# Gate and up projections of two SwiGLU feed-forwards as Strassen block products (seven multiplications for eight)

## The chip, the cores and the metric

One NeuronCore of a Trainium2 chip runs the whole program. The metric is device time in microseconds of one execution. The engines are TensorE (matmuls, "PE"; its weight loads are "PEld"), VectorE ("DVE"), ScalarE ("ACT"), GpSimd ("POOL") and SyncE ("SP", which here issues the DMAs).

## The reference

One layer on 512 prompt tokens and 8 x 8 sample tokens (576 in all), model width 1024, feed-forward width 2816, in float32:

```python
h = modulate(rms_norm(x, n1_g), sh1, sc1)
x = x + 0.5 * g1 * swiglu(h, w1_gate, w1_up, w1_down)
h = modulate(rms_norm(x, nm_g), sh2, sc2)
mix, S_new, v_rows = token_mix(h, pos0, S0, w_in, ..., w_a, w_b, w_o)
x = x + g2 * mix
h = modulate(rms_norm(x, n2_g), sh3, sc3)
x = x + 0.5 * g3 * swiglu(h, w2_gate, w2_up, w2_down)

def swiglu(h, w_gate, w_up, w_down):
    return (jax.nn.silu(h @ w_gate) * (h @ w_up)) @ w_down
```

The shifts, scales and gates (sh, sc, g) come from `silu(c) @ w_ada + b_ada`, nine vectors of 1024 per sequence. The token mix is a gated spatial MLP beside a retention, merged through w_a, w_b and w_o.

## The kernel before

Activations stand feature-major: 8 chunks k of 128 features by 576 tokens. The tokens are two halves h of H = 288. For float32 accuracy each operand is split into a high part (a cast to fp32r) and a low part (the rest): three matmuls, high-high, high-low, low-high. Weights come from HBM as raw blocks of 512 KB (`load_raw`, line 67, on SyncE's queue); `split_w` casts on ScalarE (all ScalarE work has line 96, a wrapper that can keep ScalarE in the order of the text) and subtracts on VectorE (line 77), for a few first weights on POOL. Raw, high and low tiles rotate through five buffers each.

`proj` (line 349) makes one product of 128 outputs by 288 tokens: 8 k x 3 matmuls of 128x128 by 128x288 into one PSUM bank. `ffn` runs over 22 chunks f of 128 columns in groups of 8, 6 and 8. For each chunk it makes gate and up for both halves (4 x 24 = 96 matmuls); `act` applies silu on ScalarE, multiplies on VectorE (line 412) and splits the result (line 85) into G. After a group, `w_down` is applied to its chunks (16 products) and `resid` (lines 335 to 341) adds to x. The norms of the next stage are accumulated as x becomes final, half 0 ahead of half 1 (`LAST`).

At the start, w_ada for the first shifts and scales is fetched in 32 blocks of 256 KB (`ada_first`, line 225); two features of h at a time are modulated, and the first three weights' projections take each feature as it is ready (`block`). The other 14 strips of w_ada (`ada_strip`; matmuls in line 180, transposes 191, loads 207) run as side work between FFN 1's products: `tick` lets a generator go on after so much main work.

Between the stages, x goes to HBM (x1d) and back, w_in's first weights are fetched ahead of the end of FFN 1 and spread among the x1d stores on SyncE, and w_o's follow w_a's. The scheduler orders each engine by the text and its priorities; a transfer starts when its buffer is free and those ahead of it on SyncE have been issued.

## Time and profile before

| | us |
|---|---|
| median of 3 runs | 1774.22 |
| runs | 1772.92, 1774.22, 1774.97 |
| span of the profiled execution (its total time was not taken) | 1771.8 |
| TensorE busy | 1743.8 |
| VectorE busy | 798.6 |
| ScalarE busy | 568.3 |
| GpSimd busy | 231.6 |

The profile is one execution, and its times count from the start of the span. A group's row has the line, engine, operation, output and inputs with their shapes and the count, then busy time, mean ns of one, and the idle time before it with what ended it. A row of the stretches has start:end and length, then busy time and count of PE, PEld, DVE, ACT and POOL (with a line chosen, PE and PEld alone), the granted TensorE clock, the DMA share and GB/s. In the chain and the timeline a row has start, length, engine and line.

### The profile page before, as it was taken

Reading aid. Unit: us, or ns where it says so; the run is one execution under the profiler, and the core shown is the slowest. Engines: PE = TensorE matmul, PEld = TensorE weight load, DVE = VectorE, ACT = ScalarE, POOL = GpSimd, SP = SyncE. Lnnn points to the kernel's source line nnn. Section 1 sums busy time; section 2 is a strip of 40 time slices with the busy share of each in tenths; the row PEclk is TensorE's granted clock in tenths of the full one; section 3 lists DMA queues with packets and bytes.
Section 4 is the critical chain, followed back from the end, with each engine's and each line's share of the span. In section 5 each row is a group of like instructions: output and inputs, shape, how many; then the busy total and the mean of one; then the engine's idle time right before and its main releaser. Section 6 shows DMA issues by size and latency. Waiting matters only on the chain.

```text
span 1771.8 us, 30817 instructions
## 1 busy us (share of the span) xinstructions
PE 1743.8 (98%) x13068; PEld 1675.5 (95%) x13068; DVE 798.6 (45%) x1409; ACT 568.3 (32%) x943; POOL 231.6 (13%) x282
## 2 busy tenths in 40 slices
PE   7999999999999999999999999999999999999997
PEld 4899998999999999999999889999999999999997
DVE  4532333333366557566655654412536333343332
ACT  4422122132243433333333333322334222222233
POOL 2000000000243123022112101420042000000011
PEclk9999999999999999999999999999999999999999
DMA  9555545562333334334323333332223322132211
GB/s 310 168 162 156 167 140 169 152 185 82 120 106 102 118 110 125 108 94 123 103 87 108 101 96 110 92 120 83 82 64 85 95 84 82 56 102 84 84 37 55
DMA packets 278109, 199.55 MB, mean 113 GB/s; under 512 B 8137, under 2 KB 252105, under 8 KB 277970
## 3 DMA queue, kind: packets, MB, share of 16 engines
q1 hardware_dynamic: 277970, 197.57, 37.3%
q8 instruction: 103, 1.69, 0.4%
q14 instruction: 36, 0.29, 0.1%
HBM read 183.12 MB, written 14.42 MB: 111 GB/s over the span
## 4 chain that ended last, share of the span: by engine, by line
PE 93%; DVE 2%; DMA 2%; ACT 1%; issue 1%; POOL 1%; SPq 0%; POOLq 0%; ACTq 0%; DVEq 0%
PE ps L349 75%; PE ps L609 5%; PE ps L825 3%; PE ps L180 2%; PE ps L739 1%; PE ps L617 1%; PE ps L701 1%; DMA wraw<-in_w_down_dram 1%; PE ps L745 1%; PE ps L717 0%; DVE h L304 0%; DVE XX L312 0%; PE ps L760 0%; PE ps L472 0%; PE ps L191 0%
## 5 line engine op out<-in xcount | busy, mean ns | idle before, releaser
L349 PE MATMUL ps<-XX,whi 128*128 128x288 f32 x4864 | 983.2, 297 | 8.3 <-ACT XX L96 5.8
L349 PEld LDWEIGHTS ps<-XX,whi 128*128 128x128 f32 x4864 | 781.0, 188 | 31.1 <-issue 13.4
L349 PE MATMUL ps<-XX,wlo 128*128 128x288 f32 x2432 | 718.7, 296 | 0.0
L77 DVE TENSOR_TENSOR wlo<-wraw,whi 128x1024 fp32r<-128x1024 f32 (+1 forms) x240 | 297.3, 1244 | 437.9 <-ACT whi L96 434.0
L349 PEld LDWEIGHTS ps<-XX,wlo 128*128 128x128 f32 x2432 | 456.9, 188 | 0.0
L349 PE MATMUL ps<-c,whi 128*128 128x288 f32 x2176 | 440.5, 297 | 0.0
L96 ACT CAST whi<-wraw 128x1024 fp32r<-128x1024 f32 (+1 forms) x248 | 255.3, 1035 | 544.7 <-PE ps L349 326.6
L349 PEld LDWEIGHTS ps<-c,whi 128*128 128x128 f32 x2176 | 348.0, 188 | 9.5 <-issue 6.7
L349 PE MATMUL ps<-c,wlo 128*128 128x288 f32 x1088 | 320.7, 295 | 0.0
L349 PEld LDWEIGHTS ps<-c,wlo 128*128 128x128 f32 x1088 | 204.2, 188 | 0.0
L341 POOL TENSOR_TENSOR x<-x,s 128x64 f32<-128x64 f32 x56 | 18.5, 331 | 929.2 <-DVE s L340 929.2
L412 DVE TENSOR_TENSOR h<-ps,h 128x288 f32<-128x288 f32 x88 | 40.2, 456 | 166.9 <-PE ps L349 165.6
L96 ACT CAST c<-h 128x288 fp32r<-128x288 f32 x120 | 51.5, 432 | 160.5 <-DVE h L412 139.9
L335 DVE SCALAR_TENSOR_TENSOR x<-ps,gate,x 128x288 f32<-128x288 f32 (+1 forms) x96 | 46.2, 482 | 120.6 <-PE ps L349 120.6
L609 PE MATMUL ps<-whi,XX 128*128 128x256 f32 x512 | 91.2, 281 | 0.0
L609 PEld LDWEIGHTS ps<-whi,XX 128*128 128x128 f32 x512 | 78.6, 188 | 0.0
L96 ACT COPY c<-ps 128x64 f32<-128x64 f32 (+3 forms) x86 | 37.0, 433 | 126.6 <-PE ps L609 72.1
L609 PE MATMUL ps<-wlo,XX 128*128 128x256 f32 x256 | 71.9, 281 | 0.0
L96 ACT ACTIVATE h<-ps 128x288 f32<-128x288 f32 x104 | 42.5, 409 | 79.2 <-PE ps L349 79.0
L85 DVE TENSOR_TENSOR c<-h,c 128x288 fp32r<-128x288 f32 x120 | 54.2, 454 | 25.0 <-ACT c L96 24.9
L794 DVE TENSOR_TENSOR c<-c,ps 128x288 f32<-128x288 f32 x112 | 46.4, 448 | 33.6 <-PE ps L349 33.2
L564 POOL TENSOR_TENSOR c<-h,h 128x288 f32<-128x288 f32 x32 | 33.3, 1042 | 191.2 <-DVE h L563 191.2
(176 smaller groups left out, 1279.8 us busy)
## 6 DMA issues: line engine op xcount, KB each, us to landing
wraw<-in_w_in_dram SPq DMA_DIRECT2D x80, 512.0 KB
wraw<-in_w_ada_dram SPq DMA_DIRECT2D x56, 512.0 KB
wraw<-in_w_gate_dram SPq DMA_DIRECT2D x44, 512.0 KB
wraw<-in_w_up_dram SPq DMA_DIRECT2D x44, 512.0 KB
wraw<-in_w_down_dram SPq DMA_DIRECT2D x32, 512.0 KB
c<-in_w_ada_dram SPq DMA_DIRECT2D x32, 256.0 KB
S<-in_state_ret_dram SPq DMA_DIRECT2D x32, 256.0 KB
wraw<-in_w_b_dram SPq DMA_DIRECT2D x16, 512.0 KB
```

What stands on the lines that cost most here:

```text
L77: (eng or DVE).tensor_tensor(out=lo, in0=raw, in1=hi.bitcast(F32), op=ALU.subtract)
L85: DVE.tensor_tensor(out=lo, in0=src, in1=hi.bitcast(F32), op=ALU.subtract)
L96: inst = f(*args, **kw)
L180: PE.matmul(ps[32 * g:32 * g + 32], lhsT=cs[:, k, :], rhs=w, start=k < 4, stop=k >= 4, tile_position=(0, 32 * g))
L335: DVE.scalar_tensor_tensor(out=x[:, o:o + w], in0=ps[:, :w], scalar=g[:, c, 0:1], in1=x[:, o:o + w], op0=ALU.mult, op1=ALU.add)
L341: POOL.tensor_tensor(out=x[:, NP:T], in0=x[:, NP:T], in1=u, op=ALU.add)
L349: PE.matmul(ps[:, :H], lhsT=s[:, k, c0:c0 + P], rhs=m[:, HALF[h]], start=k == 0 and z == 0, stop=k == kc - 1 and z == 2,)
L412: DVE.tensor_tensor(out=g, in0=pu[:, :H], in1=s, op=ALU.mult)
L564: POOL.tensor_tensor(out=dst[:, HALF[h]], in0=t1, in1=t2, op=ALU.add)
L609: PE.matmul(ps[:, :DV], lhsT=s, rhs=m, start=i == 0, stop=i == 23)
L794: DVE.tensor_tensor(out=dst, in0=dst, in1=ps[:, :H], op=ALU.add)
L825: PE.matmul(ps, lhsT=s, rhs=m[:, kx % 2, :], start=kx == 0 and z == 0, stop=kx == KC - 1 and z == len(terms) - 1,)
```

## The change

Gate and up of one chunk f are taken as a 2x2 block product: block rows are gate and up, the contraction is cut into k 0 to 3 and 4 to 7, and the columns are the two token halves. In Winograd's form this needs seven block products of 4 k x 3 = 12 matmuls in place of eight: 84 per chunk. The weights are combined into sums s1 to s4 (VectorE, lines 537, 544 and 545 of the changed kernel), each combination is split (`put`, lines 526 and 527), and the products go into PSUM banks that are read in between (`snap`, on ScalarE) and added to further. VectorE subtracts the snapshots (lines 563, 578, 584) and multiplies (588, 593). The activations are combined once per FFN: N11, B21, B22, N1, T2, N3 and N4, from an unsplit h (`hb`), in `h_rows` (437), `h_samples` (448) and `x_combos` (458, 466, 467), with splits in lines 424 and 429.

The buffers change with it: the pairs of a high and a low part (`whl`) have 4 buffers in an FFN, one for each of the four splits of a pair; raw weights are 1 MB in 2 buffers, shared by gate/up and w_down; the groups are 5, 6, 5, 6. The pools of each stage are opened and closed (`reuse_waits="tile"`), so that one stage's memory is the next one's. Of the 14 ada strips, 6 run in FFN 1 and 8 in the token mix, ended by `finish()` ahead of w_o; their loads are 256 KB each. `LAST3` orders w_o's products.

```diff
-NSLOT = 30
+NSLOT = 28
+FSLOT = 12
+GROUPS = (5, 6, 5, 6)
...
+        if only != 1:
+            n1 = combo("N1", b11, b12, ALU.subtract)
+        if only != 0:
+            t2 = hbp.tile([P, 2, H], F32, tag="tx", name=nm("tx"), bufs=3)[:, 0:j1 - j0]
+            DVE.tensor_tensor(out=t2, in0=b22, in1=b12, op=ALU.subtract)
+            DVE.tensor_tensor(out=t2, in0=t2, in1=b11, op=ALU.add)
+            split_x(ops["T2"], j0, j1, t2)
+            split_x(ops["B22"], j0, j1, b22)
+            combo("N3", b12, b22, ALU.subtract)
+            combo("N4", b21, t2, ALU.subtract)
...
+    def prod(ps, w, x, fresh):
+        (wh, wl), (xh, xl) = w, x
+        for j in range(4):
+            for z, (s, m) in enumerate(((wh, xh), (wh, xl), (wl, xh))):
+                PE.matmul(
+                    ps[:, :H], lhsT=s[:, j * P:(j + 1) * P], rhs=m[:, j, :],
+                    start=fresh and j == 0 and z == 0, stop=j == 3 and z == 2, skip_group_check=True,
+                )
+        tick(cost(4))
...
+        def put(self, names, src):
+            n = len(names)
+            hl = now["hl"].tile([P, 2, n, 512], F32R, tag="whl", name=nm("whl"), bufs=4)
+            ACT.copy(out=hl[:, 0], in_=src)
+            DVE.tensor_tensor(out=hl[:, 1], in0=src, in1=hl[:, 0].bitcast(F32), op=ALU.subtract)
...
+        def split1(self):
+            self.put(("a11", "a12"), self.q[:, 0:2])
+
+        def split2(self):
+            q = self.q
+            S = self.S = now["raw"].tile([P, 2, 512], F32, tag="sum", name=nm("sum"), bufs=1)
+            DVE.tensor_tensor(
+                out=S, in0=q[:, 2:3].broadcast_to([P, 2, 512]), in1=q[:, 0:4:3], op=ALU.add
+            )
+            self.put(("s3", "s1"), S)
+
+        def split3(self):
+            q, S = self.q, self.S
+            DVE.tensor_tensor(out=S[:, 0], in0=S[:, 1], in1=q[:, 0], op=ALU.add)
+            DVE.tensor_tensor(out=S[:, 1], in0=S[:, 0], in1=q[:, 1], op=ALU.add)
+            self.put(("s2", "s4"), S)
+
+        def split4(self):
+            self.put(("a22",), self.q[:, 3:4])
+
+        def p1(self, ops):
+            self.A = bank()
+            prod(self.A, self.w["a11"], ops["N11"], True)
+            self.s1 = snap(self.A)
...
+        def e2(self):
...
+            DVE.tensor_tensor(out=g, in0=self.C[:, :H], in1=self.s1, op=ALU.subtract)
+            ACT.activation(out=g, in_=g, func=AF.Silu)
+
+        def p5(self, ops):
+            self.D = bank()
+            prod(self.D, self.w["s1"], ops["N1"], True)
+            self.s5 = snap(self.D)
+
+        def p6(self, ops, t=None):
+            prod(self.A, self.w["s2"], ops["T2"], False)
+            self.s2 = snap(self.A, t)
+
+        def p3(self, ops):
+            prod(self.D, self.w["s4"], ops["B22"], False)
...
+        def p7(self, ops):
+            prod(self.A, self.w["s3"], ops["N3"], False)
+            self.t = half()
+            DVE.tensor_tensor(out=self.t, in0=self.A[:, :H], in1=self.s5, op=ALU.subtract)
...
+        def p4(self, ops):
+            prod(self.A, self.w["a22"], ops["N4"], False)
...
+            split(self.G[0], self.G[1], self.g)
...
+        for i in range(2, FC + 1):
+            if i < FC:
+                p[i] = Pair(wg, wu, i)
+                p[i].split1()
+                p[i].split2()
+                p[i].split3()
+                p[i].split4()
+                p[i].p1(ops)
+                p[i].p2(ops)
+                p[i].e2()
+            for k in todo:
+                p[k].p4(ops)
+                G.append(p[k].G)
+            todo = [i]
+            if i < FC:
+                p[i].p5(ops)
+                p[i].p6(ops)
+            if i in ends:
+                down(ends.index(i), G)
+                G = []
+            if i < FC:
+                p[i].p3(ops)
+                p[i].p7(ops)
+                p[i].e7()
...
-    rest = start(ada_rest(range(4, 18), 5.0), 8.0)
...
+    first_gate = ada_rest(range(4, 6), 3.0)
+    rest = ada_rest(range(6, 10), 12.0)
...
+    rope = tk.tile([P, 2, T], F32, name="rope")
+    nc.sync.dma_start(out=rope, in_=a["rope"])
...
+            start(ada_rest(range(10, 18), 20.0), 20.0)
...
+    finish()
+    tok_pools.close()
```

**One chunk in the middle of an FFN.** VectorE, before: per chunk two low parts of weights (wlo), and for each half the product of gate and up (h) and the low part of it (c).

```order
L412 TENSOR_TENSOR h_16899<-ps_16901,h_16898 128x288
L85 TENSOR_TENSOR c_16872<-h_16899,c_16871 128x288
L77 TENSOR_TENSOR wlo_17120<-wraw_17117,whi_17119 128x1024
L412 TENSOR_TENSOR h_16955<-ps_16957,h_16954 128x288
L77 TENSOR_TENSOR wlo_17240<-wraw_17237,whi_17239 128x1024
L85 TENSOR_TENSOR c_16872<-h_16955,c_16871 128x288
L412 TENSOR_TENSOR h_17025<-ps_17027,h_17024 128x288
L85 TENSOR_TENSOR c_16998<-h_17025,c_16997 128x288
L77 TENSOR_TENSOR wlo_17246<-wraw_17243,whi_17245 128x1024
```

VectorE, after, one pair from the sum of its weights on (sum: weight sums; whl: high and low parts; g, h: subtractions and products; c: low part of G).

```order
L537 TENSOR_TENSOR sum_2192<-wraw_2186 128x1024
L93 TENSOR_TENSOR c_2125<-g_1971,c_2124 128x576
L527 TENSOR_TENSOR whl_2189<-wraw_2186,whl_2189 128x1024
L578 TENSOR_TENSOR g_2108<-ps_2128,sn_2155 128x288
L527 TENSOR_TENSOR whl_2194<-sum_2192,whl_2194 128x1024
L584 TENSOR_TENSOR h_2183<-ps_2072,sn_2141 128x288
L544 TENSOR_TENSOR sum_2192<-sum_2192,wraw_2186 128x512
L588 TENSOR_TENSOR g_2108<-g_2108,h_2183 128x288
L545 TENSOR_TENSOR sum_2192<-sum_2192,wraw_2186 128x512
L563 TENSOR_TENSOR g_2233<-ps_2220,sn_2218 128x288
L527 TENSOR_TENSOR whl_2199<-sum_2192,whl_2199 128x1024
L527 TENSOR_TENSOR whl_2202<-wraw_2186,whl_2202 128x512
```

ScalarE, after, the same pair: casts to whl, snapshots (sn) of PSUM banks, silu (ACTIVATE), and the cast of the previous pair's G (c).

```order
L104 CAST whl_2189<-wraw_2186 128x1024
L104 CAST c_2124<-g_1971 128x576
L104 COPY sn_2141<-ps_2128 128x288
L104 COPY sn_2155<-ps_2072 128x288
L104 CAST whl_2194<-sum_2192 128x1024
L104 ACTIVATE g_2108<-g_2108 128x288
L104 COPY sn_2218<-ps_2205 128x288
L104 CAST whl_2199<-sum_2192 128x1024
L104 CAST whl_2202<-wraw_2186 128x512
```

Six instructions per chunk became thirteen on VectorE (with that of line 593, the next row); the snapshot sn_2141, which p3 needs, stands behind the cast of G on ScalarE, which needs the product of line 593.

**From FFN 1 to the token mix.** SyncE, before: the loads of w_in stand among the stores of x (x1d).

```order
L67 DMA wraw_5109<-in_w_in_dram 128x8x128
L67 DMA wraw_5115<-in_w_in_dram 128x8x128
L541 DMA x1d<-x_12_130 128x576
L67 DMA wraw_5121<-in_w_in_dram 128x8x128
L541 DMA x1d<-x_13_131 128x576
L67 DMA wraw_5127<-in_w_in_dram 128x8x128
L541 DMA x1d<-x_14_132 128x576
L67 DMA wraw_5435<-in_w_in_dram 128x4x256
```

SyncE, after: the same loads (wraw_5012 on) stand behind the stores and behind the load of the rope table, which waits for TensorE.

```order
L812 DMA x1d<-x_7_79 128x576
L812 DMA x1d<-x_8_80 128x576
L812 DMA x1d<-x_9_81 128x576
L847 DMA rope<-in_rope_dram 128x1152
L73 DMA wraw_5012<-in_w_in_dram 128x8x128
L73 DMA wraw_5017<-in_w_in_dram 128x8x128
L73 DMA wraw_5022<-in_w_in_dram 128x8x128
L73 DMA wraw_5027<-in_w_in_dram 128x8x128
L812 DMA x1d<-x_10_82 128x576
```

All w_in loads moved behind the rope load; the last store has gone behind four of them.

**From w_a to w_o.** TensorE, before: the last matmuls with w_a (c, whi) are followed by the first with w_o (XX).

```order
L349 MATMUL ps_13418<-c_12114,whi_13324 128x288
L349 MATMUL ps_13418<-c_12115,whi_13324 128x288
L349 MATMUL ps_13418<-c_12114,wlo_13325 128x288
L349 MATMUL ps_13456<-XX,whi_13452 128x288 x2
L349 MATMUL ps_13456<-XX,wlo_13453 128x288
```

TensorE, after, ahead of the first product of w_o (ps_13556): the transposes that end one ada strip, the matmuls of the last strip and its transposes.

```order
L205 MATMUL ps_13488<-ident,c_13486 128x128 x4
L194 MATMUL ps_13496<-c_13497,cs 32x512
L194 MATMUL ps_13496<-c_13498,cs 32x512
L194 MATMUL ps_13496<-c_13503,cs 32x512
L194 MATMUL ps_13496<-c_13504,cs 32x512
L194 MATMUL ps_13496<-c_13509,cs 32x512
L194 MATMUL ps_13496<-c_13510,cs 32x512
L194 MATMUL ps_13496<-c_13515,cs 32x512
L194 MATMUL ps_13496<-c_13516,cs 32x512
L205 MATMUL ps_13523<-ident,c_13521 128x128 x4
L357 MATMUL ps_13556<-XX,wd_13553 128x288 x2
```

Twenty such ada matmuls (four of one strip, eight each of two) now stand between w_a's last product and w_o's first.

402 lines of the change are left out of this document (286 added, 116 removed).

## The prediction

> **What bounds the kernel now.** I read the page first (busy time, share of the chain), then the chain of waits in order of time, then the busy time by stretches, then the groups by shape.
>
> ```profile
> span 1771.8 us, 30817 instructions
> PE 1743.8 (98%) x13068; PEld 1675.5 (95%) x13068; DVE 798.6 (45%) x1409; ACT 568.3 (32%) x943; POOL 231.6 (13%) x282
> PE 93%; DVE 2%; DMA 2%; ACT 1%; issue 1%; POOL 1%; SPq 0%; POOLq 0%; ACTq 0%; DVEq 0%
> ```
>
> TensorE is busy for 98% of the span and makes up 93% of the chain that ended last. The chain of waits (start, length, what) shows that it never stops inside a stage:
>
> ```profile
> 69.71 0.99 PE ps L180 x8
> ...
> 394.08 95.73 PE ps L349 x720
> ...
> 1145.29 169.50 PE ps L349 x1272
> ...
> 1347.58 399.27 PE ps L349 x2999
> ```
>
> The last piece is FFN 2: 399.27 / 2999 = 0.1331 us per matmul of 128x288, and 720 in 95.73 us give 0.133 in FFN 1. I use 0.1332. The stretches (length, then busy time and count of each engine) show what stands beside it in FFN 1 and FFN 2:
>
> ```profile
> 394.00:489.00 95.00, 95.00 (x717) 95.00 (x716) 31.12 (x52) 26.33 (x44) 11.13 (x13) 1.00 0.37 109
> 1360.00:1450.00 90.00, 90.00 (x678) 90.00 (x677) 31.62 (x47) 24.35 (x41) 0.33 (x1) 1.00 0.35 100
> ```
>
> VectorE is busy a third of the time, ScalarE a quarter, DMA 0.37. So the matmul count sets the time, and there is room beside it: some 60 us in 90 on VectorE.
>
> **The matmuls removed.** Each of the 44 chunks goes from 96 to 84 matmuls: 44 x 12 = 528 fewer, 528 x 0.1332 = 70.3 us, 35.2 in each FFN. This is all on the path. If nothing else moved, 1774.2 - 70.3 = 1703.9. The rest of the sum is what takes this back.
>
> **A pair in the steady part.** The groups by shape (busy, mean ns) that price what VectorE and ScalarE now do:
>
> ```profile
> L77 DVE TENSOR_TENSOR wlo<-wraw,whi 128x1024 fp32r<-128x1024 f32 x224 | 281.8, 1264 | 406.5 <-ACT whi L96 402.8 <-DMA x<-x1d 2.8 <-PE ps L825 0.3
> L85 DVE TENSOR_TENSOR c<-h,c 128x288 fp32r<-128x288 f32 x120 | 54.2, 454 | 25.0 <-ACT c L96 24.9
> L412 DVE TENSOR_TENSOR h<-ps,h 128x288 f32<-128x288 f32 x88 | 40.2, 456 | 166.9 <-PE ps L349 165.6 <-ACT h L96 1.3
> L85 DVE TENSOR_TENSOR c<-c,c 128x576 fp32r<-128x576 f32 x16 | 12.1, 755 | 17.2 <-ACT c L96 17.2
> L304 DVE SCALAR_TENSOR_TENSOR h<-x,gain,h 128x224 f32<-128x224 f32 x12 | 5.8, 492 | 0.1
> L641 DVE TENSOR_TENSOR c<-ps,hc 128x512 f32<-128x512 f32 x8 | 5.5, 682 | 0.0
> ```
>
> ```profile
> L96 ACT CAST whi<-wraw 128x1024 fp32r<-128x1024 f32 x232 | 242.0, 1049 | 488.6 <-PE ps L349 305.0 <-DMA wraw<-in_w_gate_dram 61.8 <-issue 48.2
> L96 ACT ACTIVATE h<-ps 128x288 f32<-128x288 f32 x104 | 42.5, 409 | 79.2 <-PE ps L349 79.0
> L96 ACT CAST c<-c 128x576 fp32r<-128x576 f32 x16 | 10.8, 674 | 32.9 <-POOL c L945 23.3 <-DVE c L753 9.6
> ```
>
> Before, VectorE did 2 x 1.264 + 2 x (0.456 + 0.454) = 4.3 us per chunk. Now it does four operations of 1024 columns (three low parts, the broadcast sum) = 5.06, three of 512 (L544, L545, the low part of a22) = 2.05, five of 288 = 2.28 and the low part of G, 0.755: 10.1 us, under the 11.19 us (84 x 0.1332) that TensorE needs. By throughput it would hide. By order it does not, as I read the program order. The third weight buffer (s3, s1) has one copy per split, so the cast for the next pair starts when p7 of this pair ends. From there one chain leads to the next p7: cast 1.05, low part 1.26, p7's subtraction 0.46, L544 0.68, L588 0.46, L545 0.68, cast of s2/s4 1.05, its low part 1.26, low part of a22 0.68, L593 0.46, cast of G 0.67, snapshot of p5 0.41 (on ScalarE it stands behind the cast of G, and p3 may not add into that bank before it is read), then p3 and p7, 24 x 0.1332 = 3.20. The sum is 12.3; neighbours on VectorE overlap by nearly 0.1 each and each handing over costs 0.05, so I take 12.1. The loop is 0.9 us longer than TensorE's work. Bounds: 0 (every latency is shorter than the rows; less is impossible, TensorE has its 11.19) and 1.5 (no overlap, dearer adds). No row shows the broadcast sum; I price it as the 1024 low part. With 20 pairs after the first two, 18 us come off in FFN 2; in FFN 1 the ada strips fall partly into the gaps (8 matmuls 0.99 us, six strips left, half of it: 3), so 15.
>
> **Start of FFN 1.** Counts of L349 in three stretches, the issue of the ada blocks, and the first main matmul:
>
> ```profile
> 30.00:48.00 18.00, 10.05 (x55) 8.46 (x56) 0.81 1.10 339
> 48.00:60.00 12.00, 9.98 (x68) 9.06 (x69) 1.00 0.20 65
> 60.00:68.00 8.00, 8.00 (x62) 7.96 (x61) 1.00 0.43 120
> ```
>
> ```profile
> 18.08 19.58 SPq L225 DMA_DIRECT2D c<-in_w_ada_dram x24
> ...
> 31.80 1.09 PE ps L349 x3
> ```
>
> DMA is full until 48 (share 1.10). Before, the projections began at 31.8 on the first features, and 185 of 2112 were done at 68. Now the first product's weights are cast behind the copy of the fourth ada strip, so after all 32 ada blocks and four weight loads, and after about 19 us of VectorE work on the first six features: I get 47.7 for the first product. Then VectorE has some 17 us to do (the last two features, four 1024 and nine 576 operations) before p6 of the second pair: 10 of 14 products by 68, 120 of 1848. Left are 1728 instead of 1927, 26.5 us less and not 35.2: 8.7 lost (bounds 4 and 14). The third pair's load waits for the raw buffer of the first, until its a22 is split: 3 more (0 to 5). The same 3 at FFN 2.
>
> **FFN 1 to the token mix.** SyncE's queue, a load's way (issue, then the cast that waited for it), the POOL split, and TensorE around the change of stage:
>
> ```profile
> 453.92 3.57 SPq L67 DMA_DIRECT2D wraw<-in_w_in_dram  x2
> ```
>
> ```profile
> 211.00 0.37 SPq L67 DMA_DIRECT2D wraw<-in_w_up_dram  x1
> ...
> 214.79 1.05 ACT L96 CAST whi<-wraw 128x1024 fp32r<-128x1024 f32 x1 [5.08 <-DMA wraw<-in_w_up_dram]
> ```
>
> ```profile
> L77 POOL TENSOR_TENSOR wlo<-wraw,whi 128x1024 fp32r<-128x1024 f32 x8 | 19.6, 2447 | 15.2 <-ACT whi L96 15.1
> ```
>
> ```profile
> 20.00:40.00 20.00, 13.35 (x61) 6.19 (x56) 9.95 (x23) 5.86 (x12) 5.33 (x9) 0.83 1.10 340
> ...
> 505.00:520.00 15.00, 13.62 (x101) 13.31 (x100) 12.58 (x24) 6.37 (x14) 6.59 (x12) 1.00 0.52 157
> 520.00:530.00 10.00, 8.77 (x63) 8.20 (x61) 9.70 (x23) 6.76 (x16) 3.20 (x6) 1.00 0.32 90
> ...
> 1320.00:1340.00 20.00, 18.62 (x138) 18.32 (x137) 14.59 (x28) 12.04 (x20) 11.71 (x11) 1.00 0.22 65
> 1340.00:1360.00 20.00, 18.80 (x138) 18.41 (x138) 15.17 (x31) 11.51 (x24) 4.61 (x10) 1.00 0.15 45
> ```
>
> Before, w_in was fetched from 453.9, far ahead, and the hand-over cost 25 - 22.4 = 2.6 us of TensorE (3.4 with what lies before it). Now the token mix's memory is FFN 1's, the rope load waits for the last down product, and all w_in loads stand behind it on SyncE. Rope and 512 KB: some 5.7 us after that product, the next ones 1.7 apart (512 KB at the 340 GB/s of 20:40 is 1.5). Casts 1.05, then three POOL splits in a row, 2.45 each: 9.2, 11.7, 14.1. Those three weights are used k by k together, so TensorE stands still for 12 to 14 us, in which the norm that cost 3.4 is done: 10 lost (7 to 13).
>
> **Merge to w_o.** Before, nothing stops here (1272 matmuls in 169.5 us without a gap). Now 20 ada matmuls of the last strips stand ahead of w_o on TensorE. Twelve of the loads behind them (eleven of 256 KB, one of 1 MB, 3.8 MB) take slots that the last w_a product frees; from 3 us before its end at 340 GB/s they land 8 us after it. 8 lost (4 to 13).
>
> **Start of FFN 2.** In order of time:
>
> ```profile
> 1342.16 0.47 DVE h L295
> ...
> 1347.58 2.53 PE ps L349 x17
> ```
>
> Before, the second half's norm was ready at 1342.6 and its modulation fed the matmuls piecewise, with 40 - 37.4 = 2.6 us of TensorE lost in 1320 to 1360 (3.3 with the edges). Now only p1 and p2 of two pairs (6.4 us) need the first half alone. After the second norm VectorE has 8 rows of 224 (3.9), 20 operations of 576 columns (15.1), two of 1024 (2.5), four of 512 (2.7), nine of 288 (4.1) and four small ones: 28 us, 26 with overlap. Counted from the end of product (7,0) the norm is ready at 13.9, and the two pairs are done at about 45 with some 4 us of waiting for ScalarE and POOL, where TensorE has 32 us of work: 13 to 15 lost, 12 net (8 to 16).
>
> **The clock.** Single matmuls after the idle time at the start, and some us later:
>
> ```profile
> 35.07 0.45 PE L349 MATMUL ps<-XX,wlo 128*128 128x288 f32 x1
> 35.31 0.45 PE L349 MATMUL ps<-XX,whi 128*128 128x288 f32 x1
> ...
> 39.03 0.30 PE L349 MATMUL ps<-XX,wlo 128*128 128x288 f32 x1
> 39.16 0.43 PE L349 MATMUL ps<-XX,whi 128*128 128x288 f32 x2
> ```
>
> First they stand 0.24 us apart, later 0.13, and the granted clock of 20:40 above is 0.83. From 31.8 to about 38.6 at half pace costs 3.4 us. Two of the new pauses (token mix, w_o) are followed by dense work: up to 7; I take 4, since small matmuls break the pauses up. The pauses at the starts of the FFNs wait for VectorE, where a slower TensorE costs nothing. The Trainium skill ("TensorE: Matmul & The Clock Gate", "What's actually happening") says that the clock halves after one idle window of about 3.4 us and comes back after as much work; that speaks against a change that trades matmuls for pauses. By its figures each such pause would cost 1.7, 3.4 for two instead of my 4, and the time would come out 0.6 lower; the slow stretch above is twice as long as the page has it.
>
> **Sum.** 70.3 - (15 + 18) - 8.7 - 3 - 3 - 10 - 8 - 12 - 4 = -11.4, so 11.4 us slower. The span is 1771.8 and the median of three runs 1774.22; the 2.4 us around it I leave as they are. 1774.2 + 11.4 = 1785.6.
>
> **Rivals.** First: the loop of a pair closes in time, because neighbouring latencies overlap better than I add them; the steady 33 us are then 0 and the pauses remain: 1785.6 - 33 = 1752.6. For it: VectorE's 10.1 is under 11.19 and its rows have no waits in the sum. Against it: every step of that chain is a true dependence or ScalarE's order. It decides from 0.45 us per pair downwards (1752.6 + 40 x 0.45 = 1770.6). Second: the pauses are hidden too, 1703.9; against it is that VectorE's 26 us at FFN 2 cannot be before the norm. Third: the loop is 1.5 us too long, because the adds of sums are dearer than a low part, or a w_down split falls into it: 40 x 0.6 = 24 more, 1809.6. That the change doesn't do what it says I can exclude: the program order has 11,998 matmuls for 12,526.
>
> **Numbers.** Forecast (1772 to 1800) 0.55, first rival (1740 to 1771) 0.27, second 0.03, third 0.15. The range takes the first rival at its price and the third: 1748 to 1810. Half of each end of the unknown pauses (together about 10 up or down) lies within it. Within 0.2% (3.5 us, about what this kernel's three runs can tell apart) are 1770.7 to 1777.8, the forecast's low end: 0.10. Faster 0.31, slower 0.59.
>
> **What would show it.** Right: pairs of FFN 2 at 12.1 us, TensorE idle before p3, released by ScalarE's snapshot; about 12 us without main matmuls after FFN 1's last down product; 8 before w_o, released by DMA; VectorE close to full for 26 us at the start of FFN 2. Wrong: pairs at 11.2 with TensorE full, or pauses under half of these; then the time is under 1771.

## The result and the profile after

| | before | changed |
|---|---|---|
| median, us | 1773.76 (4 runs, 1772.92 to 1774.97) | 1796.97 (4 runs, 1792.77 to 1798.01) |
| ratio, 95% interval | | 1.0124 (1.0110 to 1.0139) |
| span of the profiled execution, us | 1771.8 | 1794.7 |

The change makes the kernel slower, by 23.2 us from median to median. The page of the changed kernel opens so:

```profile
span 1794.7 us, 30328 instructions
PE 1730.7 (96%) x12540; PEld 1619.2 (90%) x12540; DVE 1061.7 (59%) x1800; ACT 693.7 (39%) x1153; POOL 215.0 (12%) x288
PE 88%; DVE 4%; DMA 2%; ACT 2%; issue 1%; POOL 1%; SPq 0%; POOLq 0%; ACTq 0%; DVEq 0%
```

528 matmul records are gone (13,068 before, 12,540 now), but TensorE is busy only 13.1 us less (1743.8 before), and its share of the chain fell from 93% to 88%. So two things went wrong: TensorE works on something that it did not work on before, or works more slowly; and it stands still more often. The stages show where. Each stretch below runs between a first and a last main matmul, read from the trace of each kernel:

| stretch, us | before | changed | difference |
|---|---|---|---|
| start to FFN 1's first product | 31.8 | 49.3 | +17.5 |
| to FFN 1's last down product | 474.4 | 430.3 | -44.1 |
| to the token mix's first value product | 29.5 | 44.4 | +14.9 |
| to the first product of w_a | 692.8 | 716.3 | +23.5 |
| w_a | 51.0 | 58.6 | +7.6 |
| pause ahead of w_o | -0.2 | 14.0 | +14.2 |
| w_o | 51.8 | 53.7 | +1.9 |
| to FFN 2's last down product | 429.3 | 417.2 | -12.1 |
| end | 11.2 | 10.8 | -0.4 |

35.1 us of matmuls left each FFN (264 x 0.1328). FFN 2 keeps 12 us of that gain. FFN 1 with its start keeps 26.6, and part of this is only work that moved to the token mix, which grew by 31 us (with w_a) although not one of its own products changed.

**The steady loop.** A piece of the chain of waits inside FFN 2, and then one pair in the timeline (in brackets the idle time ahead, with what ended it):

```profile
1487.70 66.91 PE ps L498 x504
```

```profile
1500.27 1.76 PE L498 MATMUL ps<-XX,whl 128*128 128x288 f32 x12
1500.51 1.05 ACT L104 CAST whl<-sum 128x1024 fp32r<-128x1024 f32 x1 [1.23 <-PE ps L498]
...
1504.79 1.05 ACT L104 CAST whl<-sum 128x1024 fp32r<-128x1024 f32 x1 [0.74 <-DVE sum L545]
...
1505.04 4.95 PE L498 MATMUL ps<-XX,whl 128*128 128x288 f32 x36
...
1508.10 0.68 ACT L104 CAST c<-g 128x576 fp32r<-128x576 f32 x1 [0.22 <-DVE g L593]
1508.69 0.39 ACT L104 COPY sn<-ps 128x288 f32<-128x288 f32 x1
...
1509.84 1.75 PE L498 MATMUL ps<-xs,whl 128*128 128x288 f32 x12
...
1511.66 1.05 ACT L104 CAST whl<-sum 128x1024 fp32r<-128x1024 f32 x1 [1.23 <-PE ps L498]
```

66.91 / 504 = 0.1328 us per matmul: a pair takes 84 x 0.1328 = 11.15 us, which is also the distance of the two casts of s3 and s1 (1500.51, 1511.66), and TensorE has no gap. The forecast was 12.1. The cast at 1500.51 starts 0.24 us after the first matmul of p7 (1500.27), that is, when p3 has ended and not when p7 has. From there the chain to the end of p5's snapshot takes 8.57 us (1500.51 to 1509.08), and p3, which may start only then, starts at 1509.84 without a wait: 0.76 us to spare.

**The adaptive strips.** The 14 strips of w_ada are groups of TensorE by shape, before:

```profile
L180 PE MATMUL ps<-wraw,cs 128*32 128x512 f32 x224 | 29.8, 605 | 0.0
```

and in the changed kernel (`ada`: the six strips in FFN 1; `c`: the eight in the token mix):

```profile
L194 PE MATMUL ps<-ada,cs 128*32 128x512 f32 x96 | 30.5, 605 | 0.9 <-DMA ada<-in_w_ada_dram 0.8
L194 PE MATMUL ps<-c,cs 128*32 128x512 f32 x128 | 33.2, 618 | 4.5 <-DMA c<-in_w_ada_dram 4.5
```

The same 224 records (each of these matmuls is recorded twice), nearly the same duration of one (605 ns, in the token mix 618), and twice the busy time: 63.7 us for 29.8. Each of these matmuls uses 32 of TensorE's 128 columns, and those of different columns run side by side. The timelines show one group of before:

```profile
69.64 1.06 PE L180 MATMUL ps<-wraw,cs 128*32 128x512 f32 x8
```

and one of after:

```profile
63.65 1.05 PE L194 MATMUL ps<-ada,cs 128*32 128x512 f32 x4
```

Four matmuls together take 1.06 us, two together 1.05. The new `ada_strip` waits for two blocks of 256 KB at a time and issues their two matmuls; the old one issued four.

**The pauses.** The stretches at the start of FFN 1 and of FFN 2:

```profile
20.00:48.00 28.00, 20.39 (x82) 5.57 (x75) 21.78 (x54) 13.59 (x28) 3.07 (x8) 1.00 0.98 295
48.00:60.00 12.00, 10.26 (x63) 9.96 (x64) 10.23 (x17) 6.98 (x12) 0.00 (x0) 0.86 0.00 0
60.00:68.00 8.00, 6.86 (x41) 4.70 (x39) 7.86 (x13) 4.33 (x8) 0.00 (x0) 1.00 0.20 56
```

```profile
1357.00:1370.00 13.00, 8.92 (x64) 8.34 (x63) 9.81 (x20) 5.92 (x10) 2.99 (x4) 0.96 0.00 0
1370.00:1380.00 10.00, 9.76 (x50) 9.10 (x50) 7.45 (x16) 7.38 (x17) 2.87 (x5) 0.71 0.00 0
1380.00:1390.00 10.00, 6.00 (x25) 5.65 (x26) 9.79 (x18) 5.61 (x12) 2.18 (x6) 0.66 0.01 2
1390.00:1400.00 10.00, 5.64 (x26) 4.04 (x25) 10.00 (x17) 4.68 (x8) 0.00 (x0) 0.81 0.00 0
1400.00:1410.00 10.00, 10.00 (x65) 9.92 (x66) 6.00 (x12) 6.21 (x11) 0.00 (x0) 0.85 0.48 128
1410.00:1420.00 10.00, 7.43 (x52) 6.72 (x52) 8.53 (x11) 5.85 (x9) 0.00 (x0) 1.00 0.35 83
```

From 1357 to 1420 there are 282 matmuls; at 0.1328 us, 63 us have room for 474. The missing 192 are 25.5 us. VectorE is full from 1380 to 1400, and the granted clock is 0.66 to 0.85 from 1370 to 1410: even the fully busy stretch 1400:1410 has 65 matmuls in place of 75. Two waits of FFN 2's first matmuls, both in these stretches, stand in TensorE's waits (us in total, times, longest):

```profile
PE ps L498 <- ACT XX L104: 4.5, 2, 4.1
...
PE ps L498 <- ACT xs L104: 3.1, 1, 3.1
```

These shares are means. Taken at the edges of the trace's own clock records, the stretches show pieces at 0.50. The first lies behind FFN 1 (the second line is a part of it), the last three at the start of FFN 2:

```profile
484.87:498.52 13.65, 9.44 (x35) 8.40 (x36) 8.53 (x9) 6.42 (x9) 8.36 (x5) 0.50 1.01 276
492.00:497.00 5.00, 4.99 (x19) 4.64 (x20) 4.67 (x3) 1.05 (x1) 2.45 (x1) 0.50 1.07 322
...
1368.92:1375.75 6.83, 5.93 (x23) 5.61 (x24) 5.79 (x12) 5.77 (x13) 1.61 (x2) 0.50 0.00 0
1382.58:1389.40 6.82, 5.39 (x21) 5.05 (x22) 6.82 (x12) 4.08 (x8) 0.00 (x0) 0.50 0.01 4
1396.23:1403.06 6.83, 5.44 (x19) 4.78 (x20) 5.71 (x10) 5.18 (x10) 0.00 (x0) 0.50 0.00 0
```

From 492 to 497 TensorE is full and does 19 matmuls, 0.263 us each, twice the 0.1328. In the whole changed kernel 36.1 us of TensorE's busy time lie in such pieces, in the kernel before 5.5 us, all at its start.

After FFN 1's last down product, and ahead of w_o, the chain of waits has these pieces:

```profile
480.03 6.89 DMA wraw<-in_w_in_dram
...
486.97 1.81 POOL whl L85
...
489.58 4.86 POOL whl L85 x2
...
1297.90 7.70 DMA c<-in_w_ada_dram
...
1305.74 5.62 PE ps L194 x16
```

The first three are put down to the loads and the splits on GpSimd that the forecast named. The load is not sure, though: on ScalarE the first cast of w_in (485.85) follows the norm's modulation (485.51, 0.43 us) without a wait, so that the load had landed by then. The last two are a wait for the last blocks of the strips, and then their 16 records, alone on TensorE, one matmul after another (perhaps as their blocks land; no row here shows it). As many records that stood side by side just before them took a third of the 5.62 us:

```profile
1301.36 1.92 PE L194 MATMUL ps<-c,cs 128*32 128x512 f32 x16
```

### The profile page after: what moved, and what is told of

It reads as the page before. It is cut to its first block, busy times and chain, and to the rows that moved or that the text cites. A ratio compares the mean times of both kernels' runs of the same rounds, so it can differ in the third digit from the quotient of the medians.

```text
span 1794.7 us, 30328 instructions
## 1 busy us (share of the span) xinstructions
PE 1730.7 (96%) x12540; PEld 1619.2 (90%) x12540; DVE 1061.7 (59%) x1800; ACT 693.7 (39%) x1153; POOL 215.0 (12%) x288
## 4 chain that ended last, share of the span: by engine, by line
PE 88%; DVE 4%; DMA 2%; ACT 2%; issue 1%; POOL 1%; SPq 0%; POOLq 0%; ACTq 0%; DVEq 0%
PE ps L357 44%; PE ps L498 26%; PE ps L903 5%; PE ps L194 3%; PE ps L1119 3%; PE ps L1033 1%; PE ps L911 1%; PE ps L995 1%; PE ps L1039 1%; DMA c<-in_w_ada_dram 1%; DMA wraw<-in_w_gate_dram 1%; ACT whl L104 1%; DVE whl L527 0%; PE ps L1011 0%; PE ps L1054 0%
## 5 line engine op out<-in xcount | busy, mean ns | idle before, releaser
L357 PE MATMUL ps<-XX,whl 128*128 128x288 f32 x2688 | 372.0, 298 | 12.4 <-ACT whl L104 7.3
L357 PEld LDWEIGHTS ps<-XX,whl 128*128 128x128 f32 x2688 | 362.3, 190 | 22.9 <-ACT whl L104 7.6
L498 PE MATMUL ps<-XX,whl 128*128 128x288 f32 x2112 | 307.6, 300 | 10.5 <-ACT XX L104 4.5
L498 PEld LDWEIGHTS ps<-XX,whl 128*128 128x128 f32 x2112 | 291.8, 191 | 24.0 <-ACT XX L104 6.2
L85 DVE TENSOR_TENSOR whl<-wraw,whl 128x1024 fp32r<-128x1024 f32 x101 | 130.8, 1308 | 242.2 <-ACT whl L104 241.6
L104 ACT CAST whl<-wraw 128x1024 fp32r<-128x1024 f32 (+1 forms) x208 | 194.5, 939 | 152.3 <-PE ps L357 75.8
L357 PE MATMUL ps<-c,whl 128*128 128x288 f32 x1728 | 244.7, 298 | 0.2 <-ACT wraw L104 0.2
L498 PE MATMUL ps<-xs,whl 128*128 128x288 f32 x1584 | 234.4, 301 | 10.0 <-ACT whl L104 3.8
L498 PEld LDWEIGHTS ps<-xs,whl 128*128 128x128 f32 x1584 | 219.8, 192 | 22.8 <-issue 6.7
L357 PEld LDWEIGHTS ps<-c,whl 128*128 128x128 f32 x1728 | 232.4, 188 | 8.2 <-issue 2.7
L357 PEld LDWEIGHTS ps<-c,wd 128*128 128x128 f32 x1536 | 204.0, 188 | 4.2 <-issue 2.5
L357 PE MATMUL ps<-c,wd 128*128 128x288 f32 x1536 | 205.9, 295 | 0.0
L349 POOL TENSOR_TENSOR x<-x,s 128x64 f32<-128x64 f32 x72 | 26.6, 370 | 940.5 <-DVE s L348 935.2
L527 DVE TENSOR_TENSOR whl<-wraw,whl 128x1024 fp32r<-128x1024 f32 (+1 forms) x88 | 83.5, 951 | 11.5 <-ACT whl L104 11.4
```

The source lines that it names most:

```text
L85: (eng or DVE).tensor_tensor(out=lo, in0=raw, in1=hi.bitcast(F32), op=ALU.subtract)
L104: inst = f(*args, **kw)
L349: POOL.tensor_tensor(out=x[:, NP:T], in0=x[:, NP:T], in1=u, op=ALU.add)
L357: PE.matmul(ps[:, :H], lhsT=s[:, k, c0:c0 + P], rhs=m[:, HALF[h]], start=k == 0 and z == 0, stop=k == kc - 1 and z == 2,)
L498: PE.matmul(ps[:, :H], lhsT=s[:, j * P:(j + 1) * P], rhs=m[:, j, :], start=fresh and j == 0 and z == 0, stop=j == 3 and z == 2, skip_group ...
L527: DVE.tensor_tensor(out=hl[:, 1], in0=src, in1=hl[:, 0].bitcast(F32), op=ALU.subtract)
```

## The experiments

Ratios are against the kernel before, run beside each on the same chip. "Changed" is the changed kernel's 1796.97.

**Adaptive strips in groups of four.** Each group takes four blocks again, with half of the columns, so that the loads keep their 256 KB and the buffers stay as they are:

```diff
-        for k in range(0, KC, 2):
-            ws = [now["ada"]() for _ in range(2)]
+        for c, k in ((0, 0), (0, 4), (256, 0), (256, 4)):
+            ws = [now["ada"]().rearrange("p (k c) -> p k c", k=2) for _ in range(2)]
...
-                ada_mm(ps, k + i, w)
+                for z in range(2):
+                    ada_mm(ps[:, c:c + 256], k + 2 * i + z, w[:, z])
```

> The changed kernel, but each issue of ada matmuls takes four blocks of w_ada (columns halved, so that memory and bytes stay the same) and so all four quadrants of TensorE, in place of two. Theory P (packing): in the changed kernel a group of two ada matmuls takes 1.07 us of TensorE, as much as a group of four took before; with four groups per strip in place of two, 14 strips cost 14 x 2.1 = 30 us more. Expected: 30 us less, less what now falls into pauses (10 groups stand in the pause before w_o), so 24 to 30 us under the changed kernel, 1767 to 1773. Rival: the ada matmuls lie in gaps of TensorE or cost by columns, not by groups: 0 to 5 us less.

Measured: 1778.09 (10 runs), ratio 1.0025 (1.0015 to 1.0034), 18.9 us faster than the changed kernel. The groups by shape:

```profile
L194 PE MATMUL ps<-c,cs 128*32 128x256 f32 x256 | 24.1, 413 | 4.9 <-DMA c<-in_w_ada_dram 4.9
L194 PE MATMUL ps<-ada,cs 128*32 128x256 f32 x192 | 18.7, 391 | 1.2 <-DMA ada<-in_w_ada_dram 0.9
```

42.8 us for 63.7: 20.9 less TensorE time, nearly all of it in the run. It is less than expected because half the columns do not take half the time (391 to 413 ns for 605). FFN 1 gained 11.2 us, the token mix 7.8; the pause ahead of w_o stayed (14.3).

**The kernel before, with groups of two.** The same cause from the other side: the unchanged algorithm, with a pause in the middle of each group.

```diff
                 ada_mm(ps, 4 * kk + g, ws[g // 2][:, g % 2, :])
-            yield pause
+                if g == 1:
+                    yield pause / 2
+            yield pause / 2
```

> The kernel before, with each group of four ada matmuls of the 14 late strips issued as two groups of two, with main products between. Loads and bytes as they were. Theory P (packing): 28 more groups at 1.07 us each, 30 us slower than the kernel before (1802 to 1805). Rival (a group costs by its matmuls): 0 to 5 us slower.

Measured: 1799.69, ratio 1.0145 (1.0129 to 1.0160), +25.8 us, all of it in FFN 1 (474.4 to 499.9). The row of the strips:

```profile
L180 PE MATMUL ps<-wraw,cs 128*32 128x512 f32 x224 | 53.7, 605 | 0.0
```

53.7 for 29.8 is +23.9. So the packing alone, with no Strassen at all, costs as much as the whole change lost. The Trainium skill ("TensorEngine Tiling (Array Packing)", "Key Properties") says that tiles of the array work independently and in parallel; these rows agree: 605 ns each, and 1.06 us for four, as for two.

**A weight buffer of its own for each split.** The forecast's loop rested on the cast of s3 and s1 waiting for p7. Here each split gets a fixed buffer, so that this is really so:

```diff
-            hl = now["hl"].tile([P, 2, n, 512], F32R, tag="whl", name=nm("whl"), bufs=4)
+            home = ({"a11": "A", "s3": "B", "s2": "C", "a22": "B"}, {"a11": "D", "s3": "A", "s2": "D", "a22": "C"},
+                    {"a11": "A", "s3": "B", "s2": "C", "a22": "D"})[min(self.f, 2)][names[0]]
+            hl = now["hl"].tile([P, 2, n, 512], F32R, tag="whl" + home, name=nm("whl"), bufs=1)
...
-        return now["hl"].tile(shape, F32R, tag="whl", name=nm("whl"), bufs=4)
+        return now["hl"].tile(shape, F32R, tag="whl" + "ABCD"[c % 4], name=nm("whl"), bufs=1)
```

> The changed kernel with a fixed buffer for each of a pair's four splits, so that the cast of s3 and s1 waits for p7 of the pair before; as it is, buffers are given out in the order in which they came free, and it waits for p3, which ends 1.6 us sooner. Theory L (the forecast's latency sum was right, only the place where the loop closes was wrong): 12.1 us per pair in place of 11.15, 0.9 x 20 in each FFN, so 30 to 38 us slower, with TensorE idle ahead of p3 until ScalarE's snapshot. Rival: the latencies overlap better than the sum has them, and the loop stays under TensorE's work: 0 to 5 us slower.

Measured: 1803.38, ratio 1.0168 (1.0153 to 1.0183), +6.4 us, of which 1.5 in FFN 2 and 5.6 in FFN 1's body. ScalarE in one pair of FFN 2:

```profile
1519.41 1.05 ACT L104 CAST whl<-sum 128x1024 fp32r<-128x1024 f32 x1 [0.65 <-PE ps L498]
...
1525.64 0.40 ACT L104 COPY sn<-ps 128x288 f32<-128x288 f32 x1 [0.34 <-PE ps L498]
1526.89 0.68 ACT L104 CAST c<-g 128x576 fp32r<-128x576 f32 x1 [0.85 <-DVE g L595]
...
1530.80 1.05 ACT L104 CAST whl<-sum 128x1024 fp32r<-128x1024 f32 x1 [0.65 <-PE ps L498]
```

This pair took 11.39 us (1519.41 to 1530.80), not 12.1. The program's scheduler had put the snapshot of p5 (1525.64) ahead of the cast of G (1526.89), which shortened the chain. So I fixed that order too:

```diff
+            inst = ACT.copy(out=self.s5, in_=self.D[:, :H])
+            if self.f > 2:
+                in_order([cast[0], inst])
...
-            split(self.G[0], self.G[1], self.g)
+            cast[0] = ACT.copy(out=self.G[0], in_=self.g)
+            DVE.tensor_tensor(out=self.G[1], in0=self.g, in1=self.G[0].bitcast(F32), op=ALU.subtract)
```

> The kernel with a fixed buffer for each split (e2_own), where the scheduler also put the snapshot of p5 ahead of the cast of G; here ScalarE is made to take the cast of G first, as in the changed kernel. So this is the loop that the forecast summed: cast after p7, snapshot behind the cast of G. Theory L (the latency sum holds where the loop closes through p7): in the trace of e2_own the cast of G would end at 1527.6 and the snapshot at 1527.9 where p3 started at 1527.36, so 0.6 us per pair on top of its 11.39: 12.0 us, about 24 us more than e2_own, 1820 to 1832. Rival: the chain has slack somewhere, or the two orders cost the same: within 5 us of e2_own's 1803.

Measured: 1808.17, ratio 1.0195 (1.0179 to 1.0212), +4.8 over the one before it. The scheduler now moved other instructions of VectorE and TensorE in turn, so this is no clean test of the sum of 12.1. As a whole FFN 2 lost 1.5 and 4.9 us in the two runs, but these totals hide a gain at its start, which was not looked into: its first product came 0.5 us after w_o's last in both, and 3.1 us after it in the changed kernel. In its last 17 pairs (from the 420th matmul of gate and up to the last, down products included) FFN 2 takes 292.2 us in the changed kernel, 296.5 and 300.6 in these runs; FFN 1 takes 312.8, 319.5 and 319.6. So with p7 as the buffer's last reader a pair costs 0.25 to 0.5 us more, not 0.9.

**Rope's load behind w_in's, and w_in's low parts on VectorE.**

```diff
-    nc.sync.dma_start(out=rope, in_=a["rope"])
...
-        eng = POOL if hd == 0 else DVE
+        eng = DVE
...
+        if hd == 0:
+            nc.sync.dma_start(out=rope, in_=a["rope"])
```

> The changed kernel with the rope table's load behind the first four w_in loads on SyncE, and the low parts of the first w_in weights on VectorE in place of POOL. Theory Q (the hand-over to the token mix waits for SyncE's order and then for POOL's three low parts, 2.4 us each): the loads start when the last but one x store is issued, some 4 us sooner, and the low parts take 3.7 instead of 7.3 us: of the 44.4 us from the last down product to the first value matmul 6 to 8 go. Rival: VectorE is full with the norm there, so the low parts wait in its queue, and the loads' memory is not free sooner: 0 to 3.

Measured: 1792.08, ratio 1.0101 (1.0087 to 1.0116), 4.9 us faster. The hand-over to the token mix fell from 44.4 to 39.9. The first w_in load, though, was issued only 0.9 us earlier, and the gap of 7.3 us on TensorE after the last down product stayed: it was the splits on GpSimd that went.

**The last x1d stores behind w_in's loads as well.**

```diff
-        if h == 1:
+        if h == 1 and c < 4:
             nc.sync.dma_start(out=x1d[:, c, :], in_=xs[c])
...
         if hd == 0:
             nc.sync.dma_start(out=rope, in_=a["rope"])
+            for c in range(4, KC):
+                nc.sync.dma_start(out=x1d[:, c, :], in_=xs[c])
```

> The changed kernel with the load of rope and the last four stores of x1d issued on SyncE after the first loads of w_in, and the low parts of w_in on VectorE. Theory (the 44.4 us from the last FFN1 down product to the first value product are set by the first w_in loads, which stand on SyncE behind stores that wait for GpSimd): the first w_in load issues 4 to 6 us earlier than at 480.03, the 7.5 us wait of ScalarE for it shrinks to 2 or 3, the stretch falls to about 35 us, and the run is 9 to 10 us faster than the changed kernel, at about 1787. Rival (the loads matter little, and the stretch is set by the halved clock and by the splits themselves): the stretch stays at the 39.9 us that it had with the low parts moved alone, and the run is at about 1792.

Measured: 1791.60, ratio 1.0099 (1.0083 to 1.0114); hand-over 40.0, as without this edit. The rows of SyncE and of ScalarE:

```profile
472.83 6.04 SPq L868 DMA_DIRECT2D x1d<-x  x3
478.97 4.01 SPq L73 DMA_DIRECT2D wraw<-in_w_in_dram  x4
...
483.21 2.25 ACT L104 ACTIVATE XX<-h,mT 128x288 fp32r<-128x288 f32 x5 [1.18 <-DVE h L312]
485.37 0.43 ACT L104 ACTIVATE h<-x 128x288 f32<-128x288 f32 x1
485.70 1.98 ACT L104 CAST whl<-wraw 128x1024 fp32r<-128x1024 f32 x2
```

The scheduler put three of the four stores ahead of the loads again, so the loads did not go earlier, and the edit did not do what it was for. But the rows show that the loads are not what the first cast comes after: at 485.70 it follows ScalarE's own modulations of the norm without a wait, and those wait for VectorE (L312). What a cast ahead of those modulations would bring was not tried.

**A shorter pause for the strips of the token mix**, 12 for 20 us, so that they end before w_o:

```diff
-            start(ada_rest(range(10, 18), 20.0), 20.0)
+            start(ada_rest(range(10, 18), 12.0), 12.0)
```

> The changed kernel with a pause of 12 in place of 20 between the ada strips of the token mix, so that they end well before w_a does. Theory D: the 14 us between the last w_a product and the first w_o product, and the 3.6 us of waiting for a block before it, go; the 10 groups of ada matmuls that stood there (1.07 us each) are paid elsewhere in the token mix: 6 to 8 us less. Rival: the first w_o product then waits for its own weights or for the memory of the stage before, and nothing is won: 0 to 2.

Measured: 1798.57, ratio 1.0140 (1.0123 to 1.0157), no gain. The pause ahead of w_o fell from 14.0 to 2.45 and w_a from 58.6 to 51.0, 19.2 us together, but the stretch up to w_a grew by 21.3. Twelve groups of two moved into it (12 x 1.05 = 12.6), and they bring waits with them; the longest that I found is one of their transposes, which waits for ScalarE's copy:

```profile
1138.31 1.12 PE L205 MATMUL ps<-ident,c 128*128 128x128 f32 x4 [4.00 <-ACT c L104]
```

Behind that wait the granted clock is 0.50 from 1136.96 to 1143.79, with 5.5 us of matmuls that at the full share would take some 2.7 us less. The wait was not removed but moved.

**N4's sums and low parts and N3's low part on GpSimd** (in FFN 2's second round of operands):

```diff
-            combo("N3", b12, b22, ALU.subtract)
-            combo("N4", b21, t2, ALU.subtract)
+            combo("N3", b12, b22, ALU.subtract, None, side)
+            combo("N4", b21, t2, ALU.subtract, side, side)
...
-                x_combos(ops, hb, hbp, j, j + 2, 1)
+                x_combos(ops, hb, hbp, j, j + 2, 1, POOL)
```

> The changed kernel with six of the 576-column operations on the inputs of FFN 2 (the sum and low part of N4, the low part of N3) on POOL in place of VectorE. Theory V (the start of FFN 2 waits for VectorE's row of small operations): 6 x 0.67 = 4 us less from the end of w_o to the end. Rival: the waits are for ScalarE's casts, or POOL (about 1.9 us each by its 288-column rows) becomes last: 0, or up to 4 us more.

Measured: 1799.29, ratio 1.0144 (1.0129 to 1.0158), +2.3 us; FFN 2's part +2.1. GpSimd was slower than the wait that it took away. That leaves open whether VectorE is the bound there, so the next one takes the work away.

**The low parts of T2, N3 and N4 left out** in that round.

```diff
-            DVE.tensor_tensor(out=lo, in0=src, in1=hi.bitcast(F32), op=ALU.subtract)
+            if low:
+                DVE.tensor_tensor(out=lo, in0=src, in1=hi.bitcast(F32), op=ALU.subtract)
...
-                x_combos(ops, hb, hbp, j, j + 2, 1)
+                x_combos(ops, hb, hbp, j, j + 2, 1, False)
```

> The changed kernel without the low parts of T2, N3 and N4 in the second round of FFN2's operands: 6 subtractions of VectorE of about 0.67 us (4.0 us in all) are left out, and the products read what these buffers held before, so part of the computation is missing. Theory (at the start of FFN2 TensorE waits for VectorE, which is busy all the time from 1380 to 1400): the part from the last w_o product to the last down product of FFN2, 417.2 us, gets shorter by about 4 us, and the run by as much, to about 1793. Rival (ScalarE's casts or the clock set that start): it changes by less than 1 us.

Measured: 1789.53, ratio 1.0087 (1.0073 to 1.0101), 7.4 us faster by the medians; FFN 2's part 409.5 for 417.2, 7.7 less (the stages ahead of it moved by 3 us the other way in this profile). The stretches of its start:

```profile
1370.00:1380.00 10.00, 6.91 (x35) 6.33 (x36) 7.97 (x17) 7.79 (x17) 1.96 (x3) 0.83 0.00 0
1380.00:1390.00 10.00, 5.44 (x31) 4.97 (x30) 9.68 (x20) 5.86 (x11) 3.44 (x8) 0.87 0.01 2
1390.00:1400.00 10.00, 7.66 (x40) 6.38 (x38) 9.56 (x15) 7.04 (x12) 0.00 (x0) 0.84 0.00 1
1400.00:1410.00 10.00, 10.00 (x70) 9.79 (x71) 6.54 (x12) 5.85 (x12) 0.00 (x0) 0.95 0.77 208
```

Some 4.0 us of VectorE's work (six subtractions, each 0.67 us from its start to the next) brought 7.7. VectorE does bound this start. A part of the 7.7 is the clock: the granted share is 0.83 to 0.95 where it was 0.66 to 0.85, and the pieces at 0.50 in FFN 2's first 60 us hold 10.2 us of TensorE's work, where in the changed kernel they hold 20.2. At half the time for these 10 us, that is 5 us at most, by estimate; it was not measured by itself.

**All four together** (groups of four, rope and low parts, pause 12, GpSimd):

> The changed kernel with the edits of e1_four (all four quadrants), e3b (rope and VectorE), e4 (pause 12) and e5 (POOL) together. With groups of four the ada matmuls in the token mix cost 0.66 us, not 1.07, so that e4's 19 us of pause before w_o are bought for some 10. If the causes add: 19 from packing, 7 from the pause, 6 from the hand-over, 4 from POOL, 1797 - 36 = 1761, under both kernels. If each of the pauses only hides the next: 1772 to 1778, like e1_four alone.

Measured: 1771.05 (11 runs), ratio 0.9982 (0.9973 to 0.9992), just under the kernel before. The single effects add up to -19.9 (-18.9, -4.9, +1.6, +2.3); together they made -25.9, since strips that move into the token mix cost less once their groups are packed: the stretch up to w_a grows by 15.2 us through the pause (708.5 with packed groups alone, 723.7 here), where it grew by 21.3.

**Groups of four, the stores, and a pause of 10**, without GpSimd; the edits are those above:

> Adaptive strips in groups of four quadrants with half of the columns, the loads of rope and of the last four x1d stores behind the first w_in loads with w_in's low parts on VectorE, and a pause of 10 for the strips of the token mix. If the three causes add up: -19 for the groups, -5 to -9 for the hand-over, about 0 to -6 for the pause against the changed kernel, so 1763 to 1773, which is 0.1% to 0.6% below the kernel before. If the pause only moves the strips' time from the wait ahead of w_o into the token mix: 1770 to 1774, no different from the kernel before.

Measured: 1762.26 (5 runs), ratio 0.9931 (0.9919 to 0.9944). With the pause of 10 the stretch up to w_a is 717.1, with 12 (in the combination before) it was 723.7; why was not looked into.

**The same, with full columns in the token mix**, where slots for four blocks are free:

```diff
+        if s >= 10:
+            for k in range(0, KC, 4):
+                ws = [now["ada"]() for _ in range(4)]
...
+                yield 2 * pause
+                for i, w in enumerate(ws):
+                    ada_mm(ps, k + i, w)
```

> The kernel with the three mends, and the eight strips of the token mix in groups of four quadrants with all 512 columns, as the kernel before has them, instead of two groups with 256. A group of 512 columns takes 1.07 us and two of 256 take 1.32, so 16 groups instead of 32 save 16 x 0.25 = 4 us in the token mix: about 1759 to 1769. Rival (a strip's time beyond its matmuls, the transposes and the waits at its end, sets what it costs): within 1 us of the other.

Measured: 1758.86 (4 runs, 1758.24 to 1759.80), ratio 0.9916 (0.9902 to 0.9930): 0.84% faster than the kernel before, 38 us faster than the changed one, and 3.4 us faster than the run before it, near the 4 that the groups' price gave. Its strips:

```profile
L194 PE MATMUL ps<-ada,cs 128*32 128x256 f32 x192 | 18.7, 391 | 1.0 <-DMA ada<-in_w_ada_dram 0.9
L194 PE MATMUL ps<-c,cs 128*32 128x512 f32 x128 | 18.1, 605 | 0.0
```

The eight strips take 18.1 us of TensorE for the 33.2 of the changed kernel, with the same 128 records (605 ns each for 618).

## Why the prediction was right and wrong

The direction was right and the sum 11.8 us short (11.4 for 23.2), but that the time lies in the range is luck: two large errors nearly cancel, a cost of 33 us that is not there, and one of about 27 that was not in the sum. The first sign that I had named for being wrong, pairs at 11.2 with TensorE full, is what the trace shows; yet the time did not fall under 1771 with it, because of the second error. In us, with the strips costed at 1.05 per group of two and 1.06 per group of four:

| term | forecast | measured | from |
|---|---|---|---|
| matmuls removed | -70.3 | -70.2 | 528 x 0.1328 |
| steady loop, both FFNs | +33 | 0 | pairs at 11.15 where no strip falls in |
| strips in FFN 1 | 0 | -4.5 | 24 x 1.05 - 28 x 1.06 |
| strips in the token mix and w_a | 0 | +31.1 | 23.5 + 7.6 |
| start of FFN 1, with the raw buffer | +11.7 | +13.0 | 17.5 - 44.1 + 35.1 + 4.5 |
| FFN 1 to the token mix | +10 | +14.9 | table of the stages |
| pause and slower start at w_o | +8 | +16.1 | 14.2 + 1.9 |
| start of FFN 2, with the raw buffer | +15 | +23.0 | 35.1 - 12.1 |
| clock | +4 | in the rows above | at most 15.3, (36.1 - 5.5) / 2 |
| end | 0 | -0.4 | |
| sum | +11.4 | +23.0 | |

**Matmuls removed:** right, count and price.

**The steady loop: the failed step.** "The third weight buffer (s3, s1) has one copy per split, so the cast for the next pair starts when p7 of this pair ends." The four buffers belong to no split. They are handed out in the order in which they come free, s2/s4's is free when p3 ends, and the next s3/s1 takes that one. The cast so starts one product (12 x 0.1328 = 1.6 us) earlier than I had it. The latencies that I added were nearly right: 8.57 measured from cast to snapshot, 0.24 ahead of it and 3.2 for p3 and p7 make 12.0, my 12.1. Without p7 in the ring it is 10.4, under the 11.15 of TensorE's work, and then the overrun is nothing: a latency costs only what it has above the work that covers it. So the 33 us rested on a ring that I drew one step too long. This is the first rival's outcome, though not by its reason (the latencies overlap no better than I had them), and where I called "every step of that chain" a true dependence, its first step was none. The fixed buffers show a second error: with p7 in the ring, a pair lost 0.25 to 0.5 us and not 0.9, since the program's order, which I took as fixed, changed with it.

**The strips: the term that was missing.** I had them at "8 matmuls 0.99 us" and took their sum as unchanged by the move. The row said `x8`, which is two records for each of four matmuls that run side by side; the new program issues groups of two, and each group costs the same where main products stand between the groups. Groups of two in the kernel before (+25.8) and groups of four in the changed one (-18.9) both show it.

**Start of FFN 1:** 13.0 for 11.7; the first product came at 49.3 for my 47.7. Right, and by the cause named: DMA at 0.98 until 48 and idle after, VectorE busy 10.23 of 12 and 7.86 of 8 us.

**FFN 1 to the token mix:** under by 4.9. The GpSimd splits are as described, and without them the hand-over is 4.4 us shorter. But the loads that I put first are not what the first cast follows, in the changed kernel and in the last experiment on it: that is the norm's modulation, which ScalarE does first. The stretch holds 192 matmuls, 25.5 us. Of its 39.9 us without the GpSimd splits, 7.3 are the gap and some 2.3 the clock (4.65 us of matmuls at a share of 0.50, from 484.45 to 491.27); the other 4.8 were not taken apart. Before, it lost 4.0 in all.

**Ahead of w_o:** the wait for the strips' last blocks is there, released by DMA as written: it ends at 1305.6, 6.7 us after w_a's last product (1298.9), for my 8. I had left out what comes after it: 16 records that then run alone for 5.6 us. With the strips spread out earlier (pause 12 or 10) it is 2.45 us from w_a to w_o.

**Start of FFN 2:** the cause is right (VectorE full from 1380 to 1400, and 4 us less of its work shorten this stage by 7.7), the size too small by 8. I had counted VectorE's busy time and not what its lateness does to TensorE: the granted clock is 0.50 in pieces that hold 20.2 us of this stage's matmuls (the three shown, and one more of 3.4 us from 1420.12), and at the full share these would take half. That is up to 10 us, an estimate and an upper bound, since a part of them stands ahead of waits for VectorE. I had written that "the pauses at the starts of the FFNs wait for VectorE, where a slower TensorE costs nothing", and that does not hold: the busy stretch 1400:1410 lost 10 of its 75 matmuls at a clock of 0.85. The Trainium skill ("TensorE: Matmul & The Clock Gate", "What's actually happening") has the clock at half after about 3.4 us of idling until as much work has been done. The trace agrees in part: pieces at 0.50 begin in the waits of 3.1 and 4.1 us, but they last 6.8 us, and the third (1396.23 to 1403.06) begins behind waits of 1.7 us at most.

**The clock:** the 4 us were meant for the pauses at the token mix and at w_o. At the token mix 9.4 us of matmuls ran at 0.50, some 4.7 us more than at the full share; from 1300 to 1320, around w_o's start, the clock is 1.00. What I had at nothing, the starts of the FFNs, has the larger share. In all, the halved clock can be up to 15 of the 23 us, by the estimate in the table; no run takes it away alone.

## What to carry to other kernels

An algorithm that saves 70 us of matmuls can be worth it or not by how the side work is packed: list every group that the rewrite issues differently, and price it by what runs side by side, not by records. Before a latency ring is priced, find which release the first step really waits for (this program's pool gives out what is free first), and compare the ring with the work that covers it: near that point one step decides over everything. Price a pause with the halved clock behind it. And when an experiment takes a wait away, look at all stages, since the shorter pause at w_o alone came back in full in the token mix.

## What the runs showed of the hardware

A 32-column matmul of 128x512 in float32 has records of 605 ns whether two or four stand side by side, and the group takes 1.05 or 1.06 us. Halving its columns to 256 only brings one down to 391 to 413 ns: with them the eight strips of the token mix took 24.1 us of TensorE, with 512 columns in groups of four 18.1. In waits of 3.1, 4.1 and 7.3 us the granted clock fell to 0.50 and stayed there for 6.8 to 13.7 us, and a matmul of 128x288 then took 0.263 us for 0.1328. And work taken from VectorE ahead of a stage start came back nearly twofold (4.0 us of subtractions, 7.7 us of time), up to 5 us of it by the clock.
